# Three split weight quarters kept ready in place of two, in five slots, with the hi and lo part of an activation tile in one buffer

## The chip, the cores and the metric

The kernel runs on one core of one Trainium2 chip. A core has five engines that run their own instruction streams beside each other: TensorE (PE, matrix products), VectorE (DVE), ScalarE (ACT), GpSimd (POOL) and SyncE (SP, which here only issues transfers). The metric is the device time of one execution in microseconds (us), as the median of several runs; less is better.

## The reference

One layer of a decoder for a prompt (1024 tokens) and a sample group (8 x 8 tokens) with the same weights, in fp32. Cut to what matters here:

```python
proj = jnp.einsum("bld,de->ble", x, w_in)              # 2048 -> 6672 columns
glu_a, glu_b, conv_gate, qkv, dn_gate, beta_in, decay_in, mem_q, mem_gate = jnp.split(proj, splits, axis=-1)
u = glu_a * jax.nn.sigmoid(glu_b)
hc, conv_state = causal_dwconv(u, conv_prev, conv_w)   # width 31
out_conv = jax.nn.silu(layer_norm(hc + conv_b)) * jax.nn.silu(conv_gate)
q, k, v = jnp.split(jax.nn.silu(causal_dwconv(qkv, qkv_prev, qkv_conv_w)), 3)   # width 4
o, s_final = gated_delta_rule(q, k, v, g, beta, s0)    # chunks of 64 tokens
out_dn = rms_norm(o) * jax.nn.silu(dn_gate)
out_mem = attention(mem_q, mem_k, mem_v) * jax.nn.silu(mem_gate)
mixed = jnp.concatenate([out_conv, out_dn, out_mem], axis=-1)   # 2048
y = layer_norm(DEEPNORM_ALPHA * x + jnp.einsum("ble,ed->bld", mixed, w_out))
```

Here `rms_norm` and `attention` stand for the lines that compute them. The keys and values of 256 memory tokens come from two more products with 2048 x 512 weights. Outputs are the y of both groups and the new states.

## The kernel before

**The products.** Each operand of a large product is split in two parts: hi, the value cast to fp32r (a format that PE multiplies faster than fp32), and lo, the value minus hi, also cast. A product is then three matmuls: hi by hi, lo by hi, hi by lo. The tokens are worked through in two phases: phase 0 has 576 (512 of the prompt and the 64 of the sample, in two banks of 288), phase 1 the other 512. In either, `gemm` (L1216) goes through 52 blocks of 128 output columns (t = 0 to 51; t = 0 of phase 0 stands in a loop of its own), with the activations of the phase resident in SBUF as 16 pairs of tiles `xh[k]`, `xl[k]`, made by `split_x` (L1146). Between t = 43 and 44 of phase 0 stands the memory projection `run_mem` (L1281). Then comes the output product (from L1515), with the mixed activations in the same tiles: two groups of token tiles, each in blocks of 512 columns.

**The weights.** They are streamed. A transfer brings 512 KB, a raw tile of 128 x 1024, into one of five buffers (`load_more`, L255, keeps up to five outstanding, in the order of the list `seq`). A raw tile has two quarters of 512 columns. `split_quarter` (L289) takes the next quarter, makes the hi part `wh` on ACT (a cast) and the lo part `wl` on DVE or, for every second quarter from the 10th to the 450th, on POOL (a subtraction), in one of four slots of the pool `wp`, and appends the pair to the list `ready`. I number the quarters in this order: #1 to #176 and #209 to #240 are phase 0, #177 to #208 the memory projection, #241 to #448 phase 1, #449 to #592 the output. In phase 1 a quarter serves 12 matmuls of 512 columns, in the output 12 to 14 for most blocks. The last six quarters lie in a pool of the output phase, since the tail of the kernel holds ten quarters at once (`HOLD`).

**What sets the order.** The program is written as straight code, and each engine runs its instructions in the order in which the code issues them. `ensure(n)` (L310) splits quarters until n are ready; `gemm` and the output loop (L1541) take one off the list and call `ensure(2)`, so one quarter in use and two that are ready or being made fill three of the slots, and the split of quarter j + 2 goes to the slot that quarter j - 2 used:

```python
    def ensure(n):
        while len(ready) < n:
            if not split_quarter():
                return
```

`split_quarter` returns False when the next tile in the load list is not a weight but an activation tile. `refill` (L1344) takes these: it replaces the x tiles in the last block of a phase, `xB` at t = 51 of phase 0, the mixed tiles `m0` at t = 51 of phase 1.

All else (short convolutions, gates, the delta rule, the wide convolution's chain `hc`, attention, layer norms) is side work: generators that `side.tick()` advances between the matmuls. Whether a generator goes on at a tick is decided by a planner (`Model`, L47, and `Proxy`, L77), which adds up costs of every instruction issued so far on clocks for the engines; a generator waits until the tiles that it needs are ready by PE's clock. So when splits move, the clocks of ACT and DVE move with them, and the side work's place between the matmuls too.

Every instruction is recorded by one helper, so nearly all rows of the profile show its line, L86, and groups are told apart by tile names: `wh`, `wl` weights; `xh`, `xl` activations; `m` projection results in PSUM, `mm` those of the memory projection, `om` those of the output product; `ps` side results in PSUM; `hc` the wide convolution's chain, `cv` the short ones; `lsum` sums for its layer norm; `oms` a copy of the sample group's attention result; `rbuf`, `S`, `ut`, `xt`, `X` steps of the delta rule; `GT`, `gtmp`, `gh` gates; `y` and `xt` in the output phase the residual and the result.

Of the kernel before, what the change touches and what calls it, by code (L numbers as in the profile page):

```python
# [9 lines left out]
F32R = mybir.dt.float32r  # L10
# [6 lines left out]
P = 128  # L17
# [4 lines left out]
LN_EPS = 1e-5  # L22
NORM_EPS = 1e-6
HOLD = 10
NSPLIT = 4 * 2 * 52 + 32 + 9 * KT
QSCALE = 128 ** -0.5
NTOK = (576, 512)
# [134 lines left out]
def hybrid_step(ctx, tc, I, O):  # L162
# [6 lines left out]

    xp = ctx.enter_context(tc.tile_pool(name="xp", bufs=1))  # L170
    rawp = ctx.enter_context(tc.tile_pool(name="rawp", bufs=5))
    wp = ctx.enter_context(tc.tile_pool(name="wp", bufs=4))
    psm = ctx.enter_context(tc.tile_pool(name="psm", bufs=4, space=PSUM))
    pss = ctx.enter_context(tc.tile_pool(name="pss", bufs=4, space=PSUM))
    drp = ctx.enter_context(tc.tile_pool(name="drp", bufs=1, space=DRAM))
# [8 lines left out]
    def nm(s):  # L184
        uid[0] += 1
        return f"{s}{uid[0]}"
# [85 lines left out]
    def take_x(kind):  # L272
        for i, (k, t) in enumerate(loaded):
            if k == kind:
                del loaded[i]
                return t
        raise RuntimeError("x not loaded")

    def done_raw(*last):
        outst[0] -= 1  # L280
        md.clk["SP"] = max(md.clk["SP"], md.ready(last))
        load_more()

    Y = {}
    ready = deque()
    cur = [None, 0]
    nsplit = [0]

    def split_quarter():  # L289
        if cur[0] is None:  # L290
            if not loaded or loaded[0][0] != "w":
                return False
            cur[0] = loaded.popleft()[1]
            cur[1] = 0
        s = cur[0][:, cur[1] * 512:(cur[1] + 1) * 512]
        nsplit[0] += 1
        wpool, tg = (Y["p"], "y") if nsplit[0] > NSPLIT - (HOLD - 4) else (wp, "")
        hi = wpool.tile([P, 512], F32R, tag="wh" + tg, bufs=4 if wpool is wp else HOLD - 4, name=nm("wh"))
        lo = wpool.tile([P, 512], F32R, tag="wl" + tg, bufs=4 if wpool is wp else HOLD - 4, name=nm("wl"))
        act.copy(out=hi, in_=s)  # L300
        eng = pool if (nsplit[0] % 2 == 0 and 8 < nsplit[0] <= 450) else dve
        eng.tensor_tensor(out=lo, in0=s, in1=hi.bitcast(F32), op=ALU.subtract)
        ready.append((hi, lo))
        cur[1] += 1
        if cur[1] == 2:
            cur[0] = None
            done_raw(hi, lo)
        return True
# [5 lines that stand above are left out]
# [829 lines left out]

    xh, xl, xfull = [None] * KT, [None] * KT, [None] * KT

    def split_x(k, src, n):  # L1146
        xfull[k] = xp.tile([P, 640], F32R, tag=f"xh{k}", name=nm("xh"))
        xh[k] = xfull[k][:, 0:n]
        xl[k] = xp.tile([P, n], F32R, tag=f"xl{k}", name=nm("xl"))
        act.copy(out=xh[k], in_=src)  # L1150
        dve.tensor_tensor(out=xl[k], in0=src, in1=xh[k].bitcast(F32), op=ALU.subtract)

    def mm3(out, wh, wl, k, sl, first, last):
        pe.matmul(out=out, lhsT=wh, rhs=xh[k][:, sl], start=first, stop=False)
        pe.matmul(out=out, lhsT=wh, rhs=xl[k][:, sl], start=False, stop=False)
        pe.matmul(out=out, lhsT=wl, rhs=xh[k][:, sl], start=False, stop=last)
# [59 lines left out]
    def gemm(p, t, prev_fin, xhook=None):  # L1216
        psl = [None] * len(BANKS[p])
        for q in range(4):
            ensure(1)
            wh, wl = ready.popleft()  # L1220
            ensure(2)
            for bi, (o, n) in enumerate(BANKS[p]):
                if psl[bi] is None:
                    psl[bi] = psm.tile([P, 512], F32, tag="m", name=nm("m"))
                for kk in range(4):
                    k = 4 * q + kk
                    cs = slice(kk * P, (kk + 1) * P)
                    mm3(psl[bi][:, 0:n], wh[:, cs], wl[:, cs], k, slice(o, o + n), k == 0, k == KT - 1)
                    if q == 0 and bi == 0 and kk == 0 and prev_fin is not None:
                        prev_fin()  # L1230
                        prev_fin = None
                    if p == 1 and kk == 1:
                        side.tick()
                side.tick()
            if xhook:
                xhook(q)
            ensure(2)
        return lambda: finish(p, t, psl)


# [103 lines left out]
    def refill(kind):  # L1344
        def hook(q):
            for k in range(4 * q, 4 * q + 4, 2):
                r = take_x(kind)
                for i in range(2):
                    split_x(k + i, r[:, 512 * i:512 * i + 512], 512)
                done_raw(xl[k + 1])  # L1350
                if kind == "m0":
                    if k == 0:
                        smp.append(take_x("ms"))
                    for i in (k, k + 1):
                        x2, src = xfull[i], smp[0][:, 64 * i:64 * i + 64]
                        act.copy(out=x2[:, 512:576], in_=src)
                        dve.tensor_tensor(out=x2[:, 576:640], in0=src, in1=x2[:, 512:576].bitcast(F32), op=ALU.subtract)
                    if k == 14:
                        done_raw(x2)
        return hook  # L1360
# [47 lines left out]
    def load_xt(g, cb, i, o, rows):  # L1408
        cs = slice(cb * 512, cb * 512 + 512)
        t = Y["p"].tile([P, 512], F32, tag="xt", bufs=6, name=nm("xt"))  # L1410
        sp.dma_start(out=t[0:rows], in_=I["xs"][:, cs] if rows == 64 else I["xp"][g * 512 + o:g * 512 + o + P, cs])
        return t
# [102 lines left out]
    for g in range(2):  # L1515
# [5 lines left out]
        for cb, idx in phases:  # L1521
# [3 lines left out]
            for n, i in enumerate(idx):  # L1525
                tag = ("mmmss" if nblk == 0 else "mmsss")[n]
                bank[i] = (psm if tag == "m" else pss).tile([P, 512], F32, tag=tag, name=nm("om"))
            last = g == 1 and cb == 3 and 3 in idx
# [11 lines left out]

            for k in range(KT - HOLD if last else KT):  # L1541
                ensure(1)
                w = ready.popleft()
                ensure(3 if last else 2)
                for i in idx:
                    out3(i, k, *w)
                side.tick()
                if nblk == 0 and k == 12:
                    open_out()
                    xt = {i: load_xt(g, cb, i, *tiles[i]) for i in idx}  # L1550
                if g == 0 and cb == 3 and k % 4 == 3:
                    nxt(k // 4)
            if last:
                held = []
                for k in range(KT - HOLD, KT):
                    ensure(1)
# [4 lines left out]
                side.drain(lambda: side.q)  # L1561
                for k in range(KT - HOLD, KT):
                    out3(3, k, *held[k - KT + HOLD])
# [92 lines left out]
```

## Time and profile before

| | us |
|---|---|
| median of 3 runs | 2072.53 (2071.78 to 2075.76) |
| the profiled execution | 2066.65 |
| its span, first to last instruction | 2064.9 |
| PE busy | 1979.0 (96%) |
| DVE busy | 1428.7 (69%) |
| ACT busy | 845.9 (41%) |
| POOL busy | 602.6 (29%) |
| mean granted TensorE clock | 0.989 of full speed |

The busy shares are means over stages with different limits. Matmuls are pipelined and their ends are modelled, so the 0.39 us that a row may give for one of 512 columns is longer than the distance at which they follow each other; idle times in front of a matmul are what the text goes by. The granted clock is given as a share of 2.4 GHz; 0.50 is 1.2 GHz, its lower level.

### The profile page before, as it was taken

To read this page: it belongs to the slowest core of one execution; us is meant where nothing else is said; L and a number is where in the kernel's file an instruction comes from. 1 tells how busy PE (TensorE), PEld (TensorE's weight loads), DVE (VectorE), ACT (ScalarE), POOL (GpSimd) and SP (SyncE) were. 2 spreads that over 40 slices of the span, in tenths; PEclk is the share of its full clock that TensorE was granted. 3 is DMA by queue.
4 is the path that set the end of the run, shared out by engine and by line. 5 is a ranking of instruction groups with operands and counts; after the bars stand their busy time and mean duration, and the time that the engine had idled before them with its cause. 6 is when DMAs were issued, how large, how long until landed. Compare 5 with 4: busy or idle time off the path is not lost.

```text
span 2064.9 us, 33208 instructions
## 1 busy us (share of the span) xinstructions
PE 1979.0 (96%) x12156; PEld 1715.8 (83%) x12156; DVE 1428.7 (69%) x3190; ACT 845.9 (41%) x2013; POOL 602.6 (29%) x680
## 2 busy tenths in 40 slices
PE   8999999999999989989999999999989999999995
PEld 7999999999999969977777887787767788877784
DVE  6778877887789984245787776779985433348447
ACT  5444444444433335364444444443326522235124
POOL 5434333443323342113333333322322100006003
PEclk9999999999999999999999999999999999999998
DMA  6232233323223255354332223332232463345444
GB/s 205 84 107 83 97 97 102 93 81 105 90 88 107 96 168 171 108 176 149 96 92 90 74 89 103 102 92 82 90 101 92 153 203 106 106 160 181 142 131 144
DMA packets 107267, 239.50 MB, mean 116 GB/s; under 512 B 32224, under 2 KB 36576, under 8 KB 106848
## 3 DMA queue, kind: packets, MB, share of 16 engines
q1 hardware_dynamic: 107104, 237.39, 36.3%
q8 instruction: 95, 1.56, 0.3%
q14 instruction: 68, 0.56, 0.1%
HBM read 210.24 MB, written 27.10 MB: 115 GB/s over the span
## 4 chain that ended last, share of the span: by engine, by line
PE 36%; DVE 13%; issue 2%; ACT 2%; POOL 1%; DMA 1%; SPq 0%; POOLq 0%; DVEq 0%; ACTq 0%
PE om L86 17%; PE m L86 16%; PE ps L86 4%; DVE hc L86 4%; DVE cv L86 2%; DVE wl L86 2%; DVE y L86 1%; DVE xt L86 1%; DVE X L86 1%; DMA raw<-mx 0%; ACT wh L86 0%; ACT L86 0%; POOL wl L86 0%; POOL y L86 0%; DMA mvs<-out_mem_v_dram 0%
## 5 line engine op out<-in xcount | busy, mean ns | idle before, releaser
L86 PE MATMUL m<-xh,wh 128*128 128x288 f32 (+1 forms) x2496 | 859.4, 344 | 3.6 <-ACT wh L86 3.5
L86 PE MATMUL m<-xh,wl 128*128 128x288 f32 (+1 forms) x2496 | 819.8, 328 | 12.3 <-DVE wl L86 9.6
L86 PE MATMUL m<-xl,wh 128*128 128x288 f32 (+1 forms) x2496 | 816.4, 327 | 0.0
L86 ACT CAST wh<-raw 128x512 fp32r<-128x512 f32 x592 | 359.5, 619 | 398.9 <-PE om L86 221.4
L86 POOL TENSOR_TENSOR wl<-raw,wh 128x512 fp32r<-128x512 f32 x221 | 307.3, 1391 | 728.1 <-ACT wh L86 687.1
L86 PEld LDWEIGHTS m<-xh,wl 128*128 128x128 f32 x2496 | 469.3, 188 | 54.3 <-DVE wl L86 15.1
L86 PEld LDWEIGHTS m<-xh,wh 128*128 128x128 f32 x2496 | 470.5, 188 | 47.0 <-issue 11.1
L86 PEld LDWEIGHTS m<-xl,wh 128*128 128x128 f32 x2496 | 470.9, 189 | 30.2 <-issue 2.7
L86 DVE TENSOR_TENSOR wl<-raw,wh 128x512 fp32r<-128x512 f32 x371 | 283.2, 769 | 264.7 <-ACT wh L86 264.1
L86 DVE SCALAR_TENSOR_TENSOR hc<-u,cvc,hc 128x512 f32<-128x512 f32 x360 | 243.8, 721 | 3.1
L86 PE MATMUL om<-wl,xh 128*128 128x512 f32 x576 | 227.8, 395 | 10.3 <-DVE wl L86 9.2
L86 PE MATMUL om<-wh,xh 128*128 128x512 f32 x576 | 227.4, 395 | 3.9 <-ACT wh L86 2.7
L86 PE MATMUL om<-wh,xl 128*128 128x512 f32 x512 | 201.7, 394 | 0.0
L86 DVE TENSOR_TENSOR xt<-mb,X 128x8 f32<-128x8 f32 (+30 forms) x496 | 183.0, 369 | 11.8
L86 DVE SCALAR_TENSOR_TENSOR cv<-xr,qcw,cv 128x512 f32<-128x512 f32 (+1 forms) x216 | 167.1, 774 | 7.7
L86 POOL TENSOR_TENSOR y<-y,lnb 128x512 f32<-128x512 f32 (+1 forms) x32 | 51.7, 1639 | 342.6 <-DVE y L86 222.9
L86 PEld LDWEIGHTS om<-wl,xh 128*128 128x128 f32 x576 | 109.6, 190 | 37.8 <-DVE wl L86 13.7
L86 PEld LDWEIGHTS om<-wh,xh 128*128 128x128 f32 x576 | 109.5, 190 | 28.8 <-ACT wh L86 3.8
L86 ACT ACT_TABLE_LOAD x89 | 114.2, 1283 | 44.4 <-DVE smz L86 25.7
L86 DVE TENSOR_REDUCE X<-xt 128x4 f32<-128x8 f32 (+30 forms) x496 | 110.2, 222 | 10.6
L86 PEld LDWEIGHTS om<-wh,xl 128*128 128x128 f32 x512 | 97.4, 190 | 20.3
L86 ACT ACTIVATE oi<-ps,GT 128x128 f32<-128x128 f32 x56 | 20.6, 368 | 207.4 <-DVE r L86 192.8
(307 smaller groups left out, 2032.0 us busy)
## 6 DMA issues: line engine op xcount, KB each, us to landing
raw<-in_wt_dram SPq DMA_DIRECT2D x208, 512.0 KB, 3.8
raw<-in_wo_dram SPq DMA_DIRECT2D x72, 512.0 KB, 3.9
mb<-ysc SPq DMA_DIRECT2D x128, 64.0 KB, 2.2
raw<-mx SPq DMA_DIRECT2D x16, 512.0 KB, 3.9
xt<-in_xp_dram SPq DMA_DIRECT2D x32, 256.0 KB, 4.4
out_y_p_dram<-y SPq DMA_DIRECT2D x32, 256.0 KB, 2.8
raw<-in_xa_dram SPq DMA_DIRECT2D x16, 288.0 KB, 3.9
S<-in_sdelta_dram SPq DMA_DIRECT2D x16, 256.0 KB, 4.7
```

The source lines that it names most:

```text
L86: r = fn(**kw)
```

## The change

`WB = 5` is the number of weight slots. The pool `wp` has five in place of four, `gemm` and the output loop keep `WB - 2` = 3 quarters ready in place of 2 (the last block of the output had 3), and the pool of the output phase holds the last `HOLD - WB` = 5 quarters in place of 6. `run_mem` and the tail's loop still call `ensure(2)`. The split of quarter j + 3 then goes to the slot of quarter j - 2. `split_x` makes one tile of 1152 words in place of one of 640 for hi and one of up to 576 for lo, and the lo part begins at word 576, or at 640 for the mixed tiles `m0`, whose words 512 to 639 hold the sample group's hi and lo parts. Per k this is 1152 words in place of 1216; for 16 tiles it leaves 1024 words, 4 KB a partition, and a slot of hi and lo takes 4 KB.

```diff
@@ -22,6 +22,7 @@
 LN_EPS = 1e-5
 NORM_EPS = 1e-6
 HOLD = 10
+WB = 5
 NSPLIT = 4 * 2 * 52 + 32 + 9 * KT
 QSCALE = 128 ** -0.5
 NTOK = (576, 512)
@@ -169,7 +170,7 @@
 
     xp = ctx.enter_context(tc.tile_pool(name="xp", bufs=1))
     rawp = ctx.enter_context(tc.tile_pool(name="rawp", bufs=5))
-    wp = ctx.enter_context(tc.tile_pool(name="wp", bufs=4))
+    wp = ctx.enter_context(tc.tile_pool(name="wp", bufs=WB))
     psm = ctx.enter_context(tc.tile_pool(name="psm", bufs=4, space=PSUM))
     pss = ctx.enter_context(tc.tile_pool(name="pss", bufs=4, space=PSUM))
     drp = ctx.enter_context(tc.tile_pool(name="drp", bufs=1, space=DRAM))
@@ -294,9 +295,9 @@
             cur[1] = 0
         s = cur[0][:, cur[1] * 512:(cur[1] + 1) * 512]
         nsplit[0] += 1
-        wpool, tg = (Y["p"], "y") if nsplit[0] > NSPLIT - (HOLD - 4) else (wp, "")
-        hi = wpool.tile([P, 512], F32R, tag="wh" + tg, bufs=4 if wpool is wp else HOLD - 4, name=nm("wh"))
-        lo = wpool.tile([P, 512], F32R, tag="wl" + tg, bufs=4 if wpool is wp else HOLD - 4, name=nm("wl"))
+        wpool, tg = (Y["p"], "y") if nsplit[0] > NSPLIT - (HOLD - WB) else (wp, "")
+        hi = wpool.tile([P, 512], F32R, tag="wh" + tg, bufs=WB if wpool is wp else HOLD - WB, name=nm("wh"))
+        lo = wpool.tile([P, 512], F32R, tag="wl" + tg, bufs=WB if wpool is wp else HOLD - WB, name=nm("wl"))
         act.copy(out=hi, in_=s)
         eng = pool if (nsplit[0] % 2 == 0 and 8 < nsplit[0] <= 450) else dve
         eng.tensor_tensor(out=lo, in0=s, in1=hi.bitcast(F32), op=ALU.subtract)
@@ -1143,10 +1144,9 @@
 
     xh, xl, xfull = [None] * KT, [None] * KT, [None] * KT
 
-    def split_x(k, src, n):
-        xfull[k] = xp.tile([P, 640], F32R, tag=f"xh{k}", name=nm("xh"))
-        xh[k] = xfull[k][:, 0:n]
-        xl[k] = xp.tile([P, n], F32R, tag=f"xl{k}", name=nm("xl"))
+    def split_x(k, src, n, lo=576):
+        xfull[k] = xp.tile([P, 1152], F32R, tag=f"x{k}", name=nm("x"))
+        xh[k], xl[k] = xfull[k][:, 0:n], xfull[k][:, lo:lo + n]
         act.copy(out=xh[k], in_=src)
         dve.tensor_tensor(out=xl[k], in0=src, in1=xh[k].bitcast(F32), op=ALU.subtract)
 
@@ -1218,7 +1218,7 @@
         for q in range(4):
             ensure(1)
             wh, wl = ready.popleft()
-            ensure(2)
+            ensure(WB - 2)
             for bi, (o, n) in enumerate(BANKS[p]):
                 if psl[bi] is None:
                     psl[bi] = psm.tile([P, 512], F32, tag="m", name=nm("m"))
@@ -1234,7 +1234,7 @@
                 side.tick()
             if xhook:
                 xhook(q)
-            ensure(2)
+            ensure(WB - 2)
         return lambda: finish(p, t, psl)
 
 
@@ -1346,7 +1346,7 @@
             for k in range(4 * q, 4 * q + 4, 2):
                 r = take_x(kind)
                 for i in range(2):
-                    split_x(k + i, r[:, 512 * i:512 * i + 512], 512)
+                    split_x(k + i, r[:, 512 * i:512 * i + 512], 512, 640 if kind == "m0" else 576)
                 done_raw(xl[k + 1])
                 if kind == "m0":
                     if k == 0:
@@ -1541,7 +1541,7 @@
             for k in range(KT - HOLD if last else KT):
                 ensure(1)
                 w = ready.popleft()
-                ensure(3 if last else 2)
+                ensure(WB - 2)
                 for i in idx:
                     out3(i, k, *w)
                 side.tick()
```

The number of instructions stays the same on PE, DVE, POOL and SP; ACT has two more table loads. What moves is their order. Three places follow, each before and after. The helper's line is L87 in the change.

ACT, at the start of phase 1: `GT`, `gtmp` and `gh` are the gate chain; `wh_11513` and `wh_11531` are quarters #244 and #245 before, and in the change `wh_11423` and `wh_11484` are #245 and #246. Before:

```order
L86 COPY bdT_11462<-bd_11378 32x512
L86 ACTIVATE pt_11476,smz_11473<-ps_11470,smz_11473 128x256 x2
L86 ACT_TABLE_LOAD
L86 ACTIVATE GT_11490<-g_11487 128x40
L86 ACT_TABLE_LOAD
L86 ACTIVATE gtmp_11491<-gtmp_11491 128x40
L86 ACT_TABLE_LOAD
L86 ACTIVATE gtmp_11491<-gtmp_11491 128x40
L86 CAST gh_11509<-GT_11490 128x40
L86 CAST wh_11513<-raw_11263 128x512
L86 CAST wh_11531<-raw_11321 128x512
```

After:

```order
L87 COPY bdT_11421<-bd_11345 32x512
L87 CAST wh_11423<-raw_11267 128x512
L87 ACT_TABLE_LOAD
L87 ACTIVATE pt_11439,smz_11436<-ps_11433,smz_11436 128x256 x2
L87 ACT_TABLE_LOAD
L87 ACTIVATE GT_11453<-g_11450 128x40
L87 ACT_TABLE_LOAD
L87 ACTIVATE gtmp_11454<-gtmp_11454 128x40
L87 ACT_TABLE_LOAD
L87 ACTIVATE gtmp_11454<-gtmp_11454 128x40
L87 CAST gh_11472<-GT_11453 128x40
L87 CAST wh_11484<-raw_11267 128x512
```

The chain stood ahead of quarter #244 and now stands ahead of #246; #244 is cast a few instructions above this piece.

ACT, at the change from phase 1 to the output: the casts `xh` (before) and `x` (after) make the mixed tiles k = 12 to 15 in the piece before, and k = 8 to 11 in the piece after, of 512 prompt columns and 64 sample columns each; `sgate` is a gate of side work. Before, from quarter #450 to #451:

```order
L86 CAST wh_18296<-raw_18200 128x512
L86 CAST xh_18314<-raw_18276 128x512
L86 CAST xh_18318<-raw_18276 128x512
L86 CAST xh_18314<-raw_17990 128x64
L86 CAST xh_18318<-raw_17990 128x64
L86 CAST xh_18328<-raw_18290 128x512
L86 CAST xh_18332<-raw_18290 128x512
L86 CAST xh_18328<-raw_17990 128x64
L86 CAST xh_18332<-raw_17990 128x64
L86 ACTIVATE sgate_18344<-m_18161 128x512
L86 CAST wh_18352<-raw_18246 128x512
```

After, from quarter #449 to #451:

```order
L87 CAST wh_18212<-raw_18158 128x512
L87 CAST wh_18216<-raw_18158 128x512
L87 CAST x_18234<-raw_18170 128x512
L87 CAST x_18237<-raw_18170 128x512
L87 CAST x_18234<-raw_17918 128x64
L87 CAST x_18237<-raw_17918 128x64
L87 CAST x_18246<-raw_18194 128x512
L87 CAST x_18249<-raw_18194 128x512
L87 CAST x_18246<-raw_17918 128x64
L87 CAST x_18249<-raw_17918 128x64
L87 CAST wh_18258<-raw_18206 128x512
```

Quarter #450 stood between the tiles k = 8 to 11 and 12 to 15, and #451 behind all of them; now #450 stands ahead of k = 8 to 11 and #451 ahead of k = 12 to 15.

DVE, near the end of phase 1: the last part of the wide convolution's chain `hc`, before which the sums `lsum` can't be made. Before, the lo parts are those of #415, #417, #419 and #421:

```order
L86 TENSOR_TENSOR wl_17338<-raw_17151,wh_17337 128x512
L86 SCALAR_TENSOR_TENSOR hc_17229<-u_17101,cvc,hc_17229 128x512 x6
L86 TENSOR_TENSOR wl_17381<-raw_17195,wh_17380 128x512
L86 SCALAR_TENSOR_TENSOR hc_17229<-u_17101,cvc,hc_17229 128x512 x6
L86 TENSOR_TENSOR wl_17429<-raw_17236,wh_17428 128x512
L86 SCALAR_TENSOR_TENSOR hc_17229<-u_17101,cvc,hc_17229 128x512
L86 TENSOR_TENSOR wl_17471<-raw_17279,wh_17470 128x512
```

After, those of #417, #419, #421 and #423:

```order
L87 TENSOR_TENSOR wl_17329<-raw_17140,wh_17328 128x512
L87 SCALAR_TENSOR_TENSOR hc_17234<-u_17071,cvc,hc_17234 128x512 x7
L87 TENSOR_TENSOR wl_17370<-raw_17183,wh_17369 128x512
L87 SCALAR_TENSOR_TENSOR hc_17234<-u_17071,cvc,hc_17234 128x512 x6
L87 TENSOR_TENSOR wl_17421<-raw_17223,wh_17420 128x512
L87 SCALAR_TENSOR_TENSOR hc_17234<-u_17071,cvc,hc_17234 128x512 x2
L87 TENSOR_TENSOR wl_17460<-raw_17268,wh_17459 128x512
```

The end of the chain came after the lo part of #419 and now comes after that of #421. On PE, the first matmul that reads `lsum` stood in the middle of #419 and now stands at the end of #420.

## Rows read from the trace of the kernel before

**Rows 1.** Page: busy us of an engine, share of the span, instructions.

```profile
PE 1979.0 (96%) x12156; PEld 1715.8 (83%) x12156; DVE 1428.7 (69%) x3190; ACT 845.9 (41%) x2013; POOL 602.6 (29%) x680
```

**Rows 2.** PE's waits: tile waited for; total us, times, longest us.

```profile
PE mm L86 <- DVE wl L86: 9.8, 4, 4.2
PE m L86 <- DVE wl L86: 9.6, 13, 1.7
PE om L86 <- DVE wl L86: 9.2, 6, 5.3
PE ps L86 <- DVE rbuf L86: 5.6, 9, 1.2
...
PE m L86 <- ACT wh L86: 3.5, 2, 2.6
PE ps L86 <- DVE S L86: 3.3, 3, 2.2
PE om L86 <- ACT wh L86: 2.7, 2, 2.4
PE m L86 <- POOL wl L86: 2.6, 4, 1.1
...
PE ps L86 <- DVE ut L86: 2.4, 5, 0.5
```

**Rows 3.** Page, groups: busy us, mean ns of one; then idle before, releaser.

```profile
L86 ACT CAST wh<-raw 128x512 fp32r<-128x512 f32 x592 | 359.5, 619 | 398.9 <-PE om L86 221.4
...
L86 DVE TENSOR_TENSOR wl<-raw,wh 128x512 fp32r<-128x512 f32 x371 | 283.2, 769 | 264.7 <-ACT wh L86 264.1
```

**Rows 4.** Windows: us, busy us (instructions) of PE, PEld, DVE, ACT, POOL; clock, DMA, GB/s.

```profile
720.00:765.00 45.00, 35.19 (x129) 26.65 (x128) 42.03 (x63) 15.02 (x26) 21.27 (x15) 0.89 0.50 160
...
925.00:935.00 10.00, 8.11 (x28) 5.58 (x29) 3.88 (x9) 5.25 (x13) 2.78 (x3) 0.83 0.51 139
...
1470.00:1535.00 65.00, 57.85 (x242) 44.28 (x241) 63.26 (x73) 16.62 (x27) 19.51 (x14) 1.00 0.32 98
...
1645.00:1660.00 15.00, 11.50 (x40) 8.08 (x39) 8.12 (x18) 6.83 (x17) 1.46 (x1) 0.89 0.83 270
...
1895.00:1905.00 10.00, 8.17 (x29) 6.25 (x29) 10.00 (x9) 2.10 (x4) 8.15 (x6) 0.83 0.48 151
...
1920.00:1925.00 5.00, 5.00 (x23) 4.11 (x23) 0.69 (x1) 0.79 (x2) 0.00 (x0) 1.00 0.33 115
...
2030.00:2045.00 15.00, 12.72 (x50) 8.65 (x49) 14.77 (x15) 7.56 (x13) 10.04 (x7) 1.00 0.23 88
```

**Rows 5.** Timeline, DVE and PE, 115 to 127: start, us, operation, idle before and releaser.

```profile
115.55 5.00 DVE L86 SCALAR_TENSOR_TENSOR cv<-xr,qcw,cv 128x512 f32<-128x512 f32 x3
...
126.57 0.40 PE L86 MATMUL m<-xh,wl 128*128 128x288 f32 x1 [1.73 <-DVE wl L86]
```

**Rows 6.** Timeline, PE and ACT, 905 to 928.

```profile
906.96 0.44 PE L86 MATMUL ps<-ident,oms 128*128 128x128 f32 x2 [2.45 <-ACT oms L86]
...
926.04 1.13 ACT L86 CAST wh<-raw 128x512 fp32r<-128x512 f32 x2
...
926.71 0.79 PE L86 MATMUL m<-xh,wh 128*128 128x512 f32 x1 [2.60 <-ACT wh L86]
```

**Rows 7.** Timeline, ACT and PE, 1647 to 1653.

```profile
1647.94 1.43 ACT L86 CAST xh<-raw 128x512 fp32r<-128x512 f32 x4 [2.15 <-DMA raw<-mx]
...
1652.80 0.50 PE L86 MATMUL om<-wh,xh 128*128 128x512 f32 x1 [2.41 <-ACT wh L86]
```

**Rows 8.** Timeline, DVE and PE, 1897 to 1915.

```profile
1897.29 3.43 DVE L86 TENSOR_TENSOR wl<-raw,wh 128x512 fp32r<-128x512 f32 x2
...
1901.25 0.68 DVE L86 TENSOR_TENSOR wl<-raw,wh 128x512 fp32r<-128x512 f32 x1
...
1913.07 0.69 DVE L86 SCALAR_TENSOR_TENSOR y<-xt,om 128x512 f32<-128x512 f32 x1 [0.93 <-DMA out_y_p_dram<-y]
...
1914.41 0.80 PE L86 MATMUL om<-wl,xh 128*128 128x512 f32 x1 [5.27 <-DVE wl L86]
```

## The prediction

> **What bounds the kernel now.** First the busy times: TensorE (PE) is busy for 1979.0 us of a span of 2064.9, 96%; VectorE (DVE) is next with 1428.7, 69% [rows 1]. So time can only come out of the rest of PE's span, and out of stretches where its matmuls run at the lower clock. The second view is what PE waits for. Six rows are waits for a weight quarter: for the lo part from DVE 9.8 + 9.6 + 9.2, from GpSimd (POOL) 2.6, for the hi part from ScalarE (ACT) 3.5 + 2.7, together 37.4 us [rows 2]. This is all that weights made earlier can give back directly. Splitting takes no long time by itself: a cast is 0.62 us, a subtraction on DVE 0.77 [rows 3], and PE works 12 x 0.217 = 2.6 us on a quarter (23 matmuls in 5.00 us at full clock from 1920 on [rows 4]). Two ready quarters thus cover some 5 us. The waits arise only where the engine that splits is late by more than that, so the third view is the timeline of those places, and the fourth the windows around them with clock and busy times.
>
> The change lets every split stand one quarter earlier in the order. I go by place; each gain is a wait on PE, plus the half clock that follows it.
>
> **A, start of phase 0 (126.57).** PE waits 1.73 us for a lo part; DVE had three cv operations that took 5.00 us together ahead of it, and behind them small xt and X steps up to the split [rows 5]. In the new order this split stands ahead of the last five of those and of Y, some 3 us of DVE's time and so more than the wait: gain 1.7.
>
> **B, phase 1, POOL's lo parts.** Four waits, 2.6 us, longest 1.1 [rows 2]. One quarter earlier is 2.6 us more slack than the longest wait: I take the two in phase 1, 1.6.
>
> **T, from phase 0 to phase 1 (905 to 935).** PE waits 2.45 us for oms, which ACT makes behind x casts, and 2.60 for the hi part of quarter #244 [rows 6]. That cast stands in ACT's order behind the gate chain (table loads, GT, gtmp, gh) and begins at 926.04, right behind gh. In the new order the casts of #244 and #245 stand ahead of the chain, and #246 stands behind it, needed two quarters (5.2 us) later. The matmul that reads oms moves behind quarter #241, 2.6 us later, which covers its 2.45. After the wait the granted clock is 0.83 over 10 us [rows 4]: another 1.7 us. Gain 2.45 + 2.60 + 1.7 = 6.7. It is 3 if the chain starts later because of the casts ahead of it and #246 becomes the late one.
>
> **D, mixed tiles replace x (1645 to 1660).** ACT's casts of the mixed tiles wait for their DMA 2.15 us at 1647.94, and the hi part behind them comes 2.41 us late at 1652.80 [rows 7]. The window has PE busy 11.50 of 15 us at a clock of 0.89 [rows 4]: 3.5 idle plus 1.6 for the clock. In the new order #450 stands before the casts of the tiles k 8 to 11 and #451 before those of k 12 to 15, so they no longer wait behind these DMAs. Gain 5.1; 3 if PE then waits for the mixed tiles themselves.
>
> **C, end of phase 1 (1470 to 1535).** PE is busy 57.85 of 65 us, DVE 63.26 [rows 4]: DVE is the bound here, with the chain of hc operations, and its end releases lsum (POOL), a matmul and four evictions. A split that stands earlier takes its time from that chain. In the new order the lsum matmul stands 18 matmuls later (end of quarter #420, was the middle of #419), 18 x 0.217 = 3.9 us of PE work. DVE has, counted from its last idle moment ahead of this, 83 hc to do where it had 79, and one more wl. In this window it does 73 operations in 63.26 us, 0.87 each, so 5 x 0.87 = 4.3. The small waits of 7.15 us go, and one wait of about that length at lsum comes. Cost 0.4; bounds: 4 gained if PE's work ahead of lsum covers more, 3 lost if the long wait is followed by half clock.
>
> **E, output phase (1895 to 1920).** PE waits 5.27 us at 1914.41 for #531's lo part, which stands behind y operations that wait 0.93 us for an output DMA [rows 8]. The new order puts #531 ahead of these, and #532 takes its place: the wait moves one quarter later, 2.6, and DVE has one more wl ahead, 0.7. Gain 1.9, and what a smaller wait ahead of it gives back only arrives at the same place. Bounds: 0, and 5.3 if #532 comes before the DMA's wait.
> By the row, wl is 0.77 on average, but the pair at 1897.29 took 3.43, so 1.7 each, in a window with POOL busy 8.15 of 10 us [rows 4, 8]. The Trainium skill ("SBUF — State Buffer", Who interferes with whom) says that a DVE instruction with two SBUF inputs contends with a GpSimd instruction that reads SBUF; this pair agrees. By that rule, an extra split that stands among POOL's y additions costs 1.7, E gains 2.6 - 1.7 = 0.9, and the sum comes out 1.0 us later. I keep 0.7: the split of the next block that has the neighbours #531 now gets took 0.68, at 1901.25 [rows 8].
>
> **F, last blocks (2030 to 2045).** PE is idle 15 - 12.72 = 2.28 us, DVE busy 14.77 of 15 [rows 4]. Weights one earlier save some of it, but DVE still ends last: 1.0 (0 to 2.3).
>
> **G, memory projection (720 to 765).** Its loop keeps asking for two quarters. DVE is busy 42.03 of 45 us [rows 4], and the longest of PE's waits for DVE's lo parts here is 4.2 [rows 2]. Only the work that DVE brings into it changes: 0, between 3 lost and 3 gained.
>
> **Merged tiles, pool sizes, new waits.** The x tiles hold the same values in one buffer, with the same casts, subtractions and matmuls; a matmul that reads the hi part waits for ACT alone and one that reads the lo part for DVE, as before, in the order with its waits: 0. That space holds the fifth slot. The tail's weights, five in each pool where it was four and six, are the same ten: 0. Moving splits also moves side work, since the planner's clocks for ACT and DVE change; two table loads are new on ACT. Some results will come a little late by that. The nearest rows are the small waits for rbuf, S and ut, 11.3 us in 17 [rows 2], 0.66 each; no row says how many new ones come, and I take two or three of that size, 1.5 lost. Bounds: 5 lost, and 1.5 gained, since a shift can also end a wait.
>
> **Sum.** 1.7 + 1.6 + 6.7 + 5.1 - 0.4 + 1.9 + 1.0 + 0 - 1.5 = 16.1. The profiled execution took 2066.65 us, so 2050.55; the median of the runs, 2072.53, lies 5.88 above that execution, so 2056.4 for the median. With every term at its better end (1.7 + 1.6 + 6.7 + 5.1 + 4 + 5.3 + 2.3 + 3 + 1.5 = 31.2) it would be 2041, with every term at its worse end (1.7 + 1.6 + 3 + 3 - 3 + 0 + 0 - 3 - 5 = -1.7) 2074; the ends don't all come together, and the forecast's own range is 2050 to 2064, some 7 to each side.
>
> **Rivals.**
> 1. *Waits are only handed on.* In C, E, F DVE is the bound, and A and B may come back at the next DVE result. Then T and D alone give something, half of it if their ACT order hits the same DMA and chain one quarter later: 6 - 1.5 = 4.5, so 2068 (2064 to 2077). For it: DVE's 63.26 of 65 in C [rows 4]. Against it: T and D wait for ACT, which is not full there.
> 2. *Slower: side results queue behind one more split.* Each DVE result that PE waits for in mid-chain (rbuf, S, ut, 17 waits [rows 2]) gets one more wl ahead of it, 0.77 each: 13.1 us lost. With rival 1's gain of 4.5 this is 2081. It decides from 0.26 us per wait on (4.5 / 17), and makes the kernel slower by more than 0.2% from 0.5. For it: those waits exist, so these results have no slack. Against it: the order of one wl to the next is the same in the long run, and DVE is idle 31% of the span [rows 1].
> 3. *All of it goes.* The 37.4 us of weight waits vanish, with C's and E's: 2072.5 - 37.4 = 2035 (2034 to 2050). Against it: the waits gather in a few places, and in C, F and G DVE has no idle time in which to make weights earlier, so I give it little.
> The Trainium skill ("Perfetto Trace Analysis", Optimization Strategy) says that a repeating gap on the engine that should be saturated can mean too few buffers for the next tile. By it this rival would be the likeliest; the trace shows a repeating gap in C alone.
> 4. *It does nothing.* The split routine returns at once while an activation tile stands at the front of the load list, so at T and D a third quarter may not come to be. The orders on ACT show that it does. Then 2072.
>
> **Chances.** A measurement of this kernel can tell 0.2% from no change, 4.1 us. Forecast (2050 to 2064) 0.62, rival 1 0.17, rival 2 0.09, rival 3 0.08, rival 4 0.04. Faster: 0.62 + 0.08 + 0.07 of rival 1 = 0.77; same: 0.10 + 0.04 = 0.14; slower 0.09. The range holds the forecast, the nearer part of rival 3 (0.05) and most of rival 1 (0.13), 0.80 together: 2046 to 2071.
>
> **What would show it.** PE's waits for weights fall from 37 us to some 20, nearly all in C, E and G. In T, no wait on oms or wh near 907 and 927, and PEclk 1.00 there. In D, PE's wait of 2.41 is gone, and the casts of #450 and #451 come before the last mixed tiles. In C, the small waits merge into one at lsum of 7 us or more. I am wrong if waits for rbuf, S, ut and the like grow by more than 5 us together, if T's wait comes back at #246, or if D's becomes a wait for a mixed tile.

## The result: slower by 0.6%, and where the time went

The change takes 2085.28 us, median of 4 runs (2083.85 to 2088.53), against 2072.16 for the kernel before (4 runs, 2071.35 to 2075.76): a ratio of 1.0062 (1.0045 to 1.0080). The forecast was 2056.4, and the measured time lies outside its range. The profiled execution has a span of 2083.2 us, 18.3 more than before; the medians are 13.1 apart, since the profiled execution of before lies some 5 us under its median. In the page's busy times PE has 10 us more than in [rows 1], although it runs the same matmuls:

```profile
PE 1989.2 (95%) x12156; PEld 1725.1 (83%) x12156; DVE 1409.7 (68%) x3190; ACT 847.0 (41%) x2015; POOL 588.6 (28%) x680
```

PE's waits of the change (tile, releaser, total us, times, longest us), to be held against [rows 2]:

```profile
PE mm L87 <- DVE wl L87: 11.1, 4, 4.8
PE m L87 <- DVE wl L87: 9.2, 9, 3.1
PE om L87 <- DVE wl L87: 9.1, 4, 6.7
PE ps L87 <- DVE ut L87: 9.0, 5, 3.4
PE ps L87 <- ACT ot L87: 6.9, 5, 1.5
PE ps L87 <- DVE r L87: 5.4, 5, 1.2
...
PE ps L87 <- ACT Pc L87: 3.5, 3, 1.3
...
PE m L87 <- ACT wh L87: 1.4, 1, 1.4
...
PE ps L87 <- DVE rbuf L87: 1.1, 2, 0.7
```

The waits for weights did fall, from 37.4 us in those six rows (a seventh, for POOL's lo part in the output, held 0.8 more) to 30.8 in the four that are left, and those on POOL's lo parts are gone. In their place stand waits for side results, ut, ot, r and Pc, which were small or not there; the prediction had named such growth, by more than 5 us, as a sign of being wrong. To see where, I took for each quarter the time at which the first matmul that reads its lo part starts, in both traces, and the difference of the two. A stretch's entry is how much that difference grew within it (in us, plus is slower; side matmuls can move over its ends). The column of `e_slots`, a kernel of the experiments that has the order of the kernel before but for a few splits in the last blocks, says how good an entry is: its entries reach 2.6 us, so one below 3 says little by itself.

| stretch, quarters | forecast | the change | e_defer (below) | e_slots (below) |
|---|---|---|---|---|
| phase 0, #17 to #145 | A -1.7, and part of +1.5 | +23.3 | +1.4 | -0.1 |
| G, #177 to #209 | 0 | +0.8 | +1.3 | +2.0 |
| T, #209 to #273 | -6.7 | -5.4 | -1.6 | +2.6 |
| phase 1, #273 to #401 | B -1.6, and part of +1.5 | +10.3 | +4.0 | +2.2 |
| C, #401 to #433 | +0.4 | -4.2 | +2.3 | -2.6 |
| D, #449 to #465 | -5.1 | -6.1 | -6.4 | +0.2 |
| E, #513 to #545 | -1.9 | -2.8 | -3.8 | -2.6 |
| F, #577 to the end | -1.0 | -2.4 | -2.0 | -0.4 |

At the end it is the 18.3 us of the spans; what the table doesn't hold lies between its stretches, 3.9 of it from #433 to #449. So gains came at T and D, where the largest were forecast, and the loss is nearly all in phase 0, where next to nothing was expected, with some more in phase 1. The windows of #17 to #145, first before, then the change (columns as in [rows 4]), show what the 23.3 us consist of: PE is idle for 20.0 us in place of 6.8, and busy 10.0 us longer, with the granted clock at 0.98 in place of 1.00:

```profile
79.13:609.81 530.68, 523.91 (x4321) 505.56 (x4320) 418.14 (x1206) 227.09 (x654) 192.72 (x263) 1.00 0.30 95
```

```profile
79.59:633.52 553.93, 533.94 (x4316) 512.50 (x4315) 418.72 (x1205) 229.91 (x657) 188.90 (x264) 0.98 0.29 90
```

Two windows of the change, of the places T and D, show PE full at full clock where it was 8.11 of 10 us at 0.83 and 11.50 of 15 at 0.89:

```profile
945.00:955.00 10.00, 10.00 (x48) 8.37 (x47) 3.93 (x14) 7.00 (x14) 1.29 (x1) 1.00 0.16 52
...
1670.00:1685.00 15.00, 15.00 (x66) 11.98 (x66) 10.65 (x24) 9.45 (x23) 1.16 (x1) 1.00 0.81 251
```

PE's two longest waits for `ut` in phase 0 are 3.42 us at 464.24 and 3.29 at 250.80; here is the second. In the timeline of DVE and PE in the change, `ut` is a step of the delta rule's recurrence over the prompt, `os` and `sz` belong to that of the sample group, `cv` to a short convolution:

```profile
241.95 0.68 DVE L87 TENSOR_TENSOR wl<-raw,wh 128x512 fp32r<-128x512 f32 x1
...
243.75 0.16 DVE L87 SCALAR_TENSOR_TENSOR sz<-sz 128x1 f32<-128x1 f32 x1 [0.47 <-ACT sqs L87]
243.95 0.38 PE L87 MATMUL ps<-r,ubuf 128*128 128x128 f32 x2
...
244.59 1.31 DVE L87 TENSOR_SCALAR os<-os,sz 128x128 f32<-128x128 f32 x1 [0.68 <-POOL sz L87]
245.82 1.06 DVE L87 TENSOR_SCALAR cv<-xr,qcw 128x64 f32<-128x64 f32 x1
246.91 1.64 DVE L87 SCALAR_TENSOR_TENSOR cv<-xr,qcw,cv 128x64 f32<-128x64 f32 x3
...
249.21 1.27 DVE L87 TENSOR_TENSOR S<-S,ps 128x512 f32<-128x512 f32 x2
250.40 0.34 DVE L87 TENSOR_SCALAR ut<-ps,kz 128x128 f32<-128x128 f32 x1
...
250.80 0.79 PE L87 MATMUL ps<-ut,kd 128*128 128x128 f32 x2 [3.29 <-DVE ut L87]
```

Between 241.95 and `ut` there is one split on DVE, of 0.68 us. The product that `ut` reads (`ps<-r,ubuf`) ran at 243.95, and DVE came to `ut` only at 250.40: what makes it late is other side work in front of it. In the kernel before there is one `ut` between 226 and 262 us, at 228.84, when PE is about to begin #53; in the change there are four, from 227.65 to 262.25, the last in #58. The same four stood in #48 to #53 before. The order of the side work differs, then, and not only its distance to the splits:

```profile
228.84 0.35 DVE L86 TENSOR_SCALAR ut<-ps,kz 128x128 f32<-128x128 f32 x1 [1.22 <-PE ps L86]
```

```profile
227.65 0.35 DVE L87 TENSOR_SCALAR ut<-ps,kz 128x128 f32<-128x128 f32 x1 [1.03 <-PE ps L87]
...
262.25 0.34 DVE L87 TENSOR_SCALAR ut<-ps,kz 128x128 f32<-128x128 f32 x1
```

(the first row is of the kernel before, the other two of the change.)

### The profile page after: what moved, and what is told of

The parts are those of the page before. It is cut to its first block, busy times and chain, and to the rows that moved or that the text cites. A ratio compares the mean times of both kernels' runs of the same rounds, so it can differ in the third digit from the quotient of the medians.

```text
span 2083.2 us, 33343 instructions
## 1 busy us (share of the span) xinstructions
PE 1989.2 (95%) x12156; PEld 1725.1 (83%) x12156; DVE 1409.7 (68%) x3190; ACT 847.0 (41%) x2015; POOL 588.6 (28%) x680
## 4 chain that ended last, share of the span: by engine, by line
PE 63%; DVE 23%; issue 5%; ACT 4%; DMA 3%; POOL 2%; SPq 0%; POOLq 0%; DVEq 0%; ACTq 0%
PE m L87 35%; PE om L87 17%; PE ps L87 10%; DVE hc L87 7%; DVE cv L87 4%; DVE wl L87 3%; DVE xt L87 2%; DVE y L87 1%; ACT L87 1%; DVE X L87 1%; PE mm L87 1%; DMA raw<-in_xa_dram 1%; ACT wh L87 1%; DVE S L87 1%; DMA xsc<-X 1%
## 5 line engine op out<-in xcount | busy, mean ns | idle before, releaser
L87 PE MATMUL m<-x,wh 128*128 128x288 f32 (+1 forms) x4992 | 1233.3, 336 | 1.5 <-ACT wh L87 1.4
L87 PEld LDWEIGHTS m<-x,wh 128*128 128x128 f32 x4992 | 837.8, 190 | 73.9 <-issue 13.2
L87 PE MATMUL m<-x,wl 128*128 128x288 f32 (+1 forms) x2496 | 821.8, 329 | 9.2 <-DVE wl L87 9.2
L87 POOL TENSOR_TENSOR wl<-raw,wh 128x512 fp32r<-128x512 f32 x221 | 302.4, 1368 | 844.7 <-ACT wh L87 758.1
L87 PEld LDWEIGHTS m<-x,wl 128*128 128x128 f32 x2496 | 472.2, 189 | 47.7 <-DVE wl L87 13.1
L87 ACT CAST wh<-raw 128x512 fp32r<-128x512 f32 x592 | 360.3, 620 | 369.3 <-PE om L87 193.5
L87 DVE TENSOR_TENSOR wl<-raw,wh 128x512 fp32r<-128x512 f32 x371 | 275.0, 748 | 225.7 <-ACT wh L87 224.7
L87 PE MATMUL om<-wh,x 128*128 128x512 f32 x1088 | 343.9, 393 | 1.2 <-DVE y L87 1.2
L87 DVE SCALAR_TENSOR_TENSOR hc<-u,cvc,hc 128x512 f32<-128x512 f32 x360 | 242.3, 716 | 3.2
L87 PEld LDWEIGHTS om<-wh,x 128*128 128x128 f32 x1088 | 205.7, 189 | 45.4 <-DVE y L87 1.6
L87 PE MATMUL om<-wl,x 128*128 128x512 f32 x576 | 226.4, 393 | 9.2 <-DVE wl L87 9.1
L87 DVE TENSOR_TENSOR xt<-mb,X 128x8 f32<-128x8 f32 (+30 forms) x496 | 178.9, 361 | 11.4
L87 DVE SCALAR_TENSOR_TENSOR cv<-xr,qcw,cv 128x512 f32<-128x512 f32 (+1 forms) x216 | 159.9, 740 | 7.8
L87 POOL TENSOR_TENSOR y<-y,lnb 128x512 f32<-128x512 f32 (+1 forms) x32 | 52.9, 1674 | 330.9 <-DVE y L87 215.6
L87 PEld LDWEIGHTS om<-wl,x 128*128 128x128 f32 x576 | 109.2, 190 | 34.5 <-DVE wl L87 11.8
L87 ACT ACTIVATE oi<-ps,GT 128x128 f32<-128x128 f32 x56 | 20.6, 367 | 251.9 <-DVE r L87 250.2
L87 DVE TENSOR_REDUCE X<-xt 128x4 f32<-128x8 f32 (+30 forms) x496 | 110.0, 222 | 10.4
L87 DVE TENSOR_TENSOR x<-raw,x 128x512 fp32r<-128x512 f32 (+2 forms) x80 | 48.7, 655 | 40.6 <-ACT x L87 40.6
L87 DVE TENSOR_SCALAR cv<-xr,qcw 128x512 f32<-128x512 f32 x72 | 40.2, 558 | 35.0 <-POOL xr L87 17.4
L87 ACT ACTIVATE cv<-cv 128x512 f32<-128x512 f32 x48 | 30.3, 631 | 77.8 <-DVE cv L87 77.6
L87 ACT CAST x<-raw 128x512 fp32r<-128x512 f32 (+2 forms) x80 | 40.3, 555 | 42.8 <-PE om L87 30.0
```

What stands on the lines that cost most here:

```text
L87: r = fn(**kw)
```

## The experiments

The planner sees every split through the proxies of ACT, DVE and POOL and the raw loads through that of SP. Three things are therefore tangled in the change: the splits are earlier on the chip, the raw loads (issued when a split frees a buffer) are earlier in SP's order, and the planner answers with another order of the side work. The experiments take them apart; their theories A to D have nothing to do with the letters of the places. For that the kernels issue the real splits and loads past the planner, and charge the planner's clocks at the places where two (or three) ready quarters would have them; with the planner shown two, all side instructions on all engines stand in the order of the kernel before, row for row.

**Slots and tiles alone.** `e_slots` is the change without its earlier splits:

```diff
-            ensure(WB - 2)
+            ensure(2)
```

(three times).

> Five slots and the merged activation tiles, but two quarters ready as before; every engine's order is that of the kernel before but for a few splits in the last blocks. Theory A (the planner, whose clocks the earlier splits move, issued the side work in another order, and its results come late in phase 0): 2070 to 2074 us. Theory B (the side work's order is not at fault: each of its results queues behind one more split on DVE or ACT): 2070 to 2074 us. Theory C (the merged tile or the fifth slot itself costs, by waits or by where the tiles lie): 2080 to 2086 us.

2066.87 us, median of 12 runs, ratio to before 0.9981 (0.9969 to 0.9994). The slots and the merged tiles cost nothing: theory C falls. The time is 3 us under the range of the other theories.

**Earlier splits in the old order, and the new order without earlier splits.** `e_shadow` splits three ahead and shows the planner two; `e_neworder` splits two ahead and shows it three. In `ensure(n, m)` the first number is the chip's, the second the planner's:

```diff
-            ensure(WB - 2)
+            ensure(WB - 2, 2)     # e_shadow
+            ensure(2, WB - 2)     # e_neworder
```

> Three quarters are split early as in the change, but the planner is shown the splits where they stood before, so that all side work keeps the order of the kernel before on every engine. Theory A: the gains without the loss, 2050 to 2062 us, and no wait of PE for ut, Pc or Us over 1 us in phase 0. Theory B: as the change, 2080 to 2088 us. Theory C: 2080 to 2088 us.

> The reverse: two quarters ready as before, but the planner is shown the splits where the change has them, so that all side work has the order of the change. Theory A: as slow as the change or slower, 2084 to 2102 us, with the waits for ut, Pc and Us of the change in phase 0. Theory B: 2069 to 2075 us. Theory C: 2080 to 2086 us.

`e_shadow`: 2098.63 us, ratio 1.0134 (1.0111 to 1.0157). `e_neworder`: 2097.92 us, ratio 1.0126 (1.0100 to 1.0152). Each half alone is slower than both together. The second result is what theory A says: the new order costs without any early split, and its quarters #33 to #161 take 26.7 us longer than in e_slots. Of the waits that were expected, those for ut and Pc stand there, but none for Us:

```profile
PE ps L87 <- DVE S L87: 8.6, 11, 2.4
PE ps L87 <- DVE ut L87: 6.4, 6, 2.5
...
PE ps L87 <- ACT Pc L87: 5.7, 5, 2.2
```

It is slower than the change since it has the loss of phase 0 (25.4 us from #17 to #145) without the gains: T and D are +0.3 and +0.1 us there against before. The first contradicts theory A as I had it, since with the old order nothing should have been lost. It speaks for B by its time, but not by its waits. PE's waits in e_shadow, the first rows:

```profile
PE ps L87 <- DVE cq L87: 34.8, 8, 5.4
PE mm L87 <- DVE wl L341: 11.8, 4, 5.5
PE om L87 <- DVE wl L341: 8.0, 3, 6.9
PE m L87 <- DVE wl L341: 6.7, 7, 3.1
```

One step, `cq`, is waited for eight times: six times for 5.3 to 5.4 us and once for 2.6 in phase 0, and once for 0.2 in phase 1. It is no queue of splits: DVE was idle in front of it. The timeline of e_shadow, DVE and SP's queue (SPq):

```profile
192.15 0.17 DVE L87 TENSOR_SCALAR kzn<-kz 128x4 f32<-128x4 f32 x1
...
196.78 0.33 SPq L278 DMA_DIRECT2D raw<-in_wt_dram  x1
197.21 0.38 SPq L87 DMA_DIRECT2D xsc<-X  x1
200.78 0.37 SPq L87 DMA_DIRECT2D Uc<-xsc  x1
...
202.75 0.31 DVE L87 STREAM_TRANSPOSE Rc<-Uc 128x128 f32<-128x128 f32 x1 [6.52 <-DMA Uc<-xsc]
202.98 0.13 DVE L87 TENSOR_SCALAR cq<-cq 128x4 f32<-128x4 f32 x1
```

and of e_slots, where the step `kzn` of the same head begins at 193.12:

```profile
193.12 0.17 DVE L87 TENSOR_SCALAR kzn<-kz 128x4 f32<-128x4 f32 x1
...
193.92 0.32 SPq L87 DMA_DIRECT2D xsc<-X  x1
195.48 0.37 SPq L87 DMA_DIRECT2D Uc<-xsc  x1
197.76 0.33 SPq L87 DMA_DIRECT2D raw<-in_wt_dram  x1
...
198.20 0.30 DVE L87 STREAM_TRANSPOSE Rc<-Uc 128x128 f32<-128x128 f32 x1
```

The delta rule's small inverse goes out to DRAM and back in another shape (`xsc<-X`, `Uc<-xsc`), over SP. In e_slots `xsc<-X` is issued 0.8 us after `kzn`, and the raw load comes behind both transfers. In e_shadow the raw load stands ahead of them, since the split that it belongs to is one quarter earlier; it waits in SP's order for a split that frees its buffer, and `xsc<-X` goes out 5.1 us after `kzn`. SP's waits in the window 188 to 204 name it, 5.3 us for POOL's lo part, by line 278, the raw load:

```profile
SPq L278 <- DVE wl L341: 7.5, 1, 7.5
SPq L278 <- POOL wl L341: 5.3, 1, 5.3
```

That is theory D: a transfer that waits holds up what stands behind it in SP's order.

**Three ready at the end only.** `e_late` has `ensure(WB - 2 if p == 1 and t >= 48 else 2)` in gemm, and three in the output loop; the planner does see these splits, and no side instruction moves.

> Three quarters ready only from block 48 of phase 1 on; the side work's order is that of the kernel before everywhere. All theories but C: only the terms D, E and F can act, whose places gave 6, 4 and 0 us in the change: 2060 to 2066 us. Theory B with a price for the side results of the output phase: 2066 to 2072. Theory C: 2074 to 2080 us.

2060.04 us, ratio 0.9943 (0.9921 to 0.9965), as expected. The term D is real where neither the order nor a side transfer in SP's queue is in play: against e_slots it gains 6.6 us between #449 and #465, and 2.0 from #577 to the end (F). In E, between #513 and #545, it gains only 0.3, so that term isn't shown. (The 4 and 0 us that the expectation gives for E and F in the change are 2.8 and 2.4 in the table above, where the stretches hold the whole place.)

**Early splits, loads where they were.** `e_defer` is e_shadow with the load that a split frees issued when the planner's split, one quarter later, is done:

```diff
         if cur[1] == 2:
             cur[0] = None
-            outst[0] -= 1
-            load_more()
...
     def plan_done(last):
         soutst[0] -= 1
+        outst[0] -= 1
+        load_more()
```

`e_shadow4` leaves the loads where e_shadow has them and changes `while outst[0] < 5` to `< 4`, so that a load goes to a buffer that has been free for two quarters. `e_slots4` does the same with two quarters ready.

> As e_shadow (three quarters split early, all side work in the order of the kernel before), but the load into a raw buffer that a split frees is issued where the kernel before issued it, so that SP's order is that of the kernel before too, row by row. Theory D (SP's queue: with early splits the raw load, which waits until its buffer is split, stands ahead of the delta rule's small transfers, and these, the Uc in front of Rc and cq above all, start late): 2050 to 2062 us, and PE's waits for cq, 34.8 us in e_shadow, fall under 6. Theory B (DVE and ACT: side results queue behind one more split): 2085 to 2100 us, the waits for cq stay.

> As e_shadow, but at most four raw transfers outstanding in place of five, with five buffers: a load goes to a buffer that was freed two quarters earlier, and SP has no reason to wait for a split. Side work and its order as in the kernel before. Theory D: 2045 to 2062 us, SP's waits for wl fall from 1245 us to under 400. Theory B: 2085 to 2100 us.

> Two quarters ready as before, the order of the kernel before on PE, ACT, DVE and POOL, at most four raw transfers outstanding: what SP's waits cost in the kernel before. Theory D: 2055 to 2067 us. Theory B: 2065 to 2069 us, as e_slots, or slower, if four transfers are too few where a phase begins.

`e_defer`: 2058.52 us, ratio 0.9945 (0.9931 to 0.9958). `e_shadow4`: 2058.47 us, ratio 0.9938 (0.9922 to 0.9953). `e_slots4`: 2064.54 us, ratio 0.9970 (0.9959 to 0.9981). Theory D holds for e_shadow, twice over: with every instruction of PE, ACT, DVE and POOL in the same order, only the place of SP's loads, or only their number in flight, takes 40 us off. The wait for Rc and cq goes with it. DVE's waits for the transfer `Uc`, first e_shadow, then e_defer:

```profile
DVE Rc L87 <- DMA Uc<-xsc: 47.2, 8, 6.6
```

```profile
DVE Rc L87 <- DMA Uc<-xsc: 9.0, 9, 2.3
```

and PE's wait for cq in e_defer:

```profile
PE ps L87 <- DVE cq L87: 2.4, 2, 1.3
```

In e_shadow4 SP still waits 537.0 + 239.1 us for lo parts (896.7 + 348.4 in e_shadow), more than the 400 expected; the waits that stay are those with no side transfer behind them that matters. That e_slots4 gains little over e_slots says the same of the kernel before.

**The change itself.** `e_after4` keeps the change's order of everything but SP's loads (planner shown five outstanding, four in fact). `e_free` has four and tells the planner, `e_later` moves each load to the next split, in the change's own code, and the planner sees it:

```diff
         if cur[1] == 2:
             cur[0] = None
-            done_raw(hi, lo)
+            held_back.append((hi, lo))
...
     def split_quarter():
+        if held_back:
+            done_raw(*held_back.pop())
```

> The change, with the order of all side work exactly as the change has it (the planner is shown five outstanding transfers), but at most four raw transfers outstanding in fact. Theory A (in the change the cost is the new order itself; SP holds nothing up there, since the planner moved the delta rule's transfers away): 2080 to 2086 us, the waits for ut and Pc in phase 0 stay. Theory D (SP's queue holds the change up as it does e_shadow): 2058 to 2072 us.

> The change itself with at most four raw transfers outstanding, and the planner's clock for SP told so; the planner orders the side work anew. Theory D: 2045 to 2066 us, since neither SP nor the planner's picture of SP holds the side work up. Theory A (any new order of the side work costs some 20 us): 2075 to 2100 us. Theory B: 2080 to 2090 us.

> The change with each raw load issued at the next split in place of the one that frees its buffer; the planner sees this and orders the side work anew. Theory A (the new order comes from the earlier charge of the splits on the planner's DVE and ACT clocks, so it is much the same as in e_free): 2066 to 2086 us, with 15 us or more lost between quarters #33 and #145. Theory D: 2055 to 2064 us.

`e_after4`: 2081.01 us, ratio 1.0050 (1.0038 to 1.0063): theory A for the change. It differs from e_shadow4 in nothing but the order that the planner gave, and takes 22.5 us longer (2081.01 against 2058.47): that is the price of the order. Freeing SP gives at most some 4 us of the 27 that separate the change from e_defer, and the intervals of the change and e_after4 overlap; #33 to #161 are 19.6 us slower than in the kernel before (22.9 in the change), and the waits stay:

```profile
PE ps L87 <- DVE ut L87: 9.1, 5, 3.4
...
PE ps L87 <- ACT Pc L87: 3.5, 3, 1.3
```

`e_free`: 2071.39 us, ratio 1.0007 (0.9997 to 1.0018). `e_later`: 2062.41 us, ratio 0.9962 (0.9949 to 0.9975). Both lose much as the change does in phase 0: from #33 to #161 18.6 us more than the kernel before in either, and the recurrence's `ut` steps stand between the same quarters as in the change up to some #90. They win it back after that, 15 us from #225 to the last quarter in e_free and 19 in e_later. e_free's time lies in none of the three ranges. e_later's time lies where theory D had it and its loss in phase 0 where theory A had it: neither expectation covers it whole. Where the planner is told of later or fewer loads, it finds an order for phase 1 that is better than the change's. Why just this one, and why its clocks led it to a worse order for phase 0 in all three, is not settled.

**A third quarter in the memory projection.** `e_mem3` is e_shadow4 with `ensure(WB - 2, 2)` in `run_mem` too.

> As e_shadow4, with three quarters ready in the memory projection too. If DVE is full there, as the profile says, PE's waits for lo parts of 11.9 us stay within 2 us and the time at 2056 to 2060 us; if the third quarter was missing there, they fall under 6 us and the time to 2048 to 2054 us.

2057.17 us, ratio 0.9936 (0.9923 to 0.9948), the same as e_shadow4 within its interval. The wait stays:

```profile
PE mm L87 <- DVE wl L349: 10.4, 3, 4.9
```

DVE is the bound there, as term G said. e_defer, e_shadow4, e_mem3 and e_late are the fastest versions, 0.6% under the kernel before and 1.2 to 1.3% under the change; e_later, e_slots4 and e_slots lie between them and the kernel before.

## Why the prediction was wrong

- **The step that failed is the term "merged tiles, pool sizes, new waits".** It said that moving splits moves side work, saw that no row prices this, and took two or three small waits, 1.5 us, at most 5. The change lost 23.3 us in phase 0 and 10.3 in phase 1, so that even the sum of all worse ends, 2074 us, was passed by 11. The orders on PE and DVE are fixed before any run, and in them the recurrence has moved by some quarters in phase 0; I had priced the orders at the places with a visible wait, and nowhere else. e_neworder against e_slots, and e_after4 against e_shadow4, show that this order by itself is the loss. By what path each late result comes about is shown at 250.80 alone.
- **SP's queue was left out.** A split that moves takes its raw load along. The sum went by PE, ACT, DVE and POOL only. In the change itself this costs little (at most some 4 us, e_after4), but with the old order it costs 40 (e_shadow against e_defer).
- **T and D were right, E is not shown.** T and D gave 5.4 and 6.1 us against 6.7 and 5.1. E gave 2.8 against 1.9, and the wait did move from #531 to #532, as forecast: one of 6.69 us stands where two of 1.83 and 5.27 stood. But e_slots, without an earlier split there, gains 2.6 against the same trace of before, with a wait of 6.88 still at #531, so E's number is in part luck. The change, then e_slots:

```profile
1937.92 0.79 PE L87 MATMUL om<-wl,x 128*128 128x512 f32 x1 [6.69 <-DVE wl L87]
```

```profile
1918.46 0.79 PE L87 MATMUL om<-wl,x 128*128 128x512 f32 x1 [6.88 <-DVE wl L87]
```

- **B was right, A was not.** No row for POOL's lo parts is left among PE's waits. In A the split did move ahead, but PE waits 2.10 us where it waited 1.73: the split itself took 1.68 us there, beside a split on POOL, where the same split took 0.68 before. The short xt step in front of it took 1.38, also beside one on POOL, but so did its like before (1.35 at 123.64). Rows of DVE, POOL and PE in the change:

```profile
123.46 1.29 POOL L87 TENSOR_TENSOR wl<-raw,wh 128x512 fp32r<-128x512 f32 x1
...
123.50 1.38 DVE L87 TENSOR_TENSOR xt<-mb,X 128x116 f32<-128x116 f32 x1
...
124.98 1.26 POOL L87 TENSOR_TENSOR wl<-raw,wh 128x512 fp32r<-128x512 f32 x1 [0.23 <-ACT wh L87]
...
125.11 1.68 DVE L87 TENSOR_TENSOR wl<-raw,wh 128x512 fp32r<-128x512 f32 x1
...
126.84 0.40 PE L87 MATMUL m<-x,wl 128*128 128x288 f32 x1 [2.10 <-DVE wl L87]
```

  The rule of the Trainium skill ("SBUF — State Buffer", Who interferes with whom) that a DVE instruction with two SBUF inputs contends with a GpSimd instruction that reads SBUF bears on these rows, and they agree with it; the sum had weighed it at E and not here.

- **C was wrong in its form.** The small waits did not merge into one at lsum, which is 1.47 us; the longest is on a lo part, 3.12 us, and the stretch gained 4.2, its better bound; e_slots gains 2.6 there against the same trace, so little of it is the change's own. G moved by 0.8 us, within its bounds. F gained 2.4, 2.0 of it against e_slots, but not by the forecast way: PE's waits for lo parts there are 2.4 us in the change and 2.3 before.
- **Rival 2 had the sign and nearly the time (2081), but by luck: its mechanism is not what happened.** Its price was one more split, 0.77 us, ahead of each side result. At 250.80 no additional split stands in front of `ut`; and in e_defer, where every split is one quarter earlier in front of the same side work, PE's waits for rbuf, S and ut are 6.7 + 2.4 + 3.2 us in place of the 5.6 + 3.3 + 2.4 of [rows 2]: 1 us more, not 13. Those for Rc and cq, which hang on the transfer `Uc`, grew from 1.4 to 6.9.
- **The sum without the failed step.** e_defer is the change as I had pictured it: earlier splits, all else in place. It gains 12.6 us against before by the medians, where the sum without the 1.5 said 17.6. Even there T gave only 1.6: waits of 2.12 for ptm and 1.99 for PT stand where those for oms and wh were. The pair of traces shows 5.6, since the profiled execution of before lies under its median and that of e_defer over it.

## What to carry to other kernels

Where a planner orders work by its clocks, moving one kind of instruction is a change of the whole schedule: compare the orders everywhere, not only where a wait is to go, or hold the order fixed (charge the planner where the work stood) to see what the move itself is worth. And follow every transfer that a moved step issues: a load that waits for a buffer blocks the small transfers behind it in its queue, so issue it when its buffer is free, or keep one fewer in flight.

## What the runs showed of the hardware that was not expected

A transfer's wait is not paid by its own reader alone: in e_shadow a 512 KB weight load, whose buffer was not yet free, delayed `xsc<-X`, a transfer that had its data, by 4.3 us (issued 5.1 us after `kzn` in place of 0.8), and with the clock's fall after each wait (mean granted clock from #17 to #145 0.96 against 1.00 in e_slots) this made 6 to 7 us of every 16 quarters from #33 to #129. Having less in flight cost nothing here: four outstanding loads gave the same time as five that are issued later, 2058.5 us each.
